# A hybrid attention kernel on one core: most branch gates computed in pairs of seven half-size products

## The chip, the core and the metric

The kernel runs on one core of a Trainium2 chip. TensorE multiplies matrices into PSUM; VectorE, ScalarE and GpSimd work on tiles in SBUF; SyncE issues the loads. The metric is the device time of one execution in microseconds (us). The time before is the median of three runs.

## The reference: what is computed

Two layers of a backbone run over 640 tokens, 512 latent ones and 128 context ones, with a model width of 1024. All data is float32. In each layer

```python
h = rmsnorm(x, norm1_g) * (1 + sc1) + sh1
z = h @ w_in           # pool input, conv inputs, q, k, v, and 3 x 1024 gates
g = sigmoid(gates)     # one gate for each of three branches
merged = (g[:, :, 0] * (pool_out @ w_br_pool)
          + g[:, :, 1] * (conv_out @ w_br_conv)
          + g[:, :, 2] * (attn_out @ w_br_attn))
x = x + g1 * (merged @ w_o)
h2 = rmsnorm(x, norm2_g) * (1 + sc2) + sh2
x = x + g2 * ((silu(h2 @ w_gate) * (h2 @ w_up)) @ w_down)
```

The shifts, scales and gates sh1, sc1, g1, sh2, sc2, g2 are six slices of `silu(c) @ w_ada + b_ada`, 6 x 1024 values per layer and group of tokens.

## The kernel before

Activations lie with channels on the 128 partitions and the 640 tokens along the row, eight chunks of 128 channels. Each float32 operand is held as two parts in TensorE's input form: a rounded high part and the exact rest, the low part. A product of one weight block and one chunk is three matmuls (high by high, low by high, high by low), on two halves of 320 tokens. So a plain output block of 128 channels, eight chunks deep, takes 8 x 2 x 3 = 48 matmuls of 320 columns (`mm`, `mm_op`, L682).

In the feed-forward part, two blocks that read the same input (gate and up) are computed as a *pair* (`Pair`, `Seven`, `product`, L585): the 2 x 2 block product is formed from seven products of half size instead of eight, each 4 chunks x 3 = 12 matmuls. For it the weights are added into four sums s1 to s4 and the input into four sums t1 to t4. Of a pair's seven weight parts three (a11, a12, a22) are the loaded weights themselves and four are sums. `Quarters` holds the input side: `exact` keeps the unsplit input that the norm has just made, `combine` forms t1 to t4 from it on VectorE, and `parts` splits them.

Weights come by SyncE into four raw buffers (`RAW`), are rounded by ScalarE (L351) and get their low part from VectorE by a subtraction (L352), into six buffers `wq` (`WQ`). A plain unit of 1024 columns takes two of these, a half-size part or a branch block one. The 24 gate blocks of a layer (three branches, eight chunks) are plain units in the order `MERGE`. `Merge.gate` takes the tanh of a gate on ScalarE (L1476), multiplies it with the branch's product on VectorE (L1481), adds (L1487) and splits the sum of three (L300, L301) into four of the thirteen big buffers (`BIG`).

From the end of attention on, `ada_back` computes the modulation: for each of 48 rows of `w_ada` in layer 0 and 32 in layer 1 a load of 512 KB and two VectorE instructions with read-out (L751). Two row buffers, `av` and `ap`, lie in room that the attention's values and scores have left; the two conditioning vectors lie in the room of the keys (`k`).

The order of the instructions on every engine is fixed at build time. A planner (`_Order`) runs all these routines as tasks with estimated costs: each engine takes the waiting instruction that is due first. Main work is due at once, weight splits 1.5 us later (`WEIGHT`), weight sums 6 us later, and modulation rows (`BACK`) only where nothing else waits. On the chip each engine runs its list strictly in order.

## Time and profile before

| what | value |
|---|---|
| median of three runs | 1872.57 us (1868.22 to 1874.47) |
| profiled execution | 1872.58 us |
| its span | 1870.5 us |
| TensorE busy | 1820.7 us (97%), 12427 matmuls |
| VectorE busy | 1394.1 us (75%), 2343 instructions |
| ScalarE busy | 816.3 us (44%), 1437 instructions |
| GpSimd busy | 40.1 us (2%), 79 instructions |
| granted clock, mean of the span | 0.993 |
| DMA: bytes moved | 196.81 MB, all loads and stores issued by SyncE |

Busy time is an average over stages with different limits, so the stages are read one by one. Layer 0 ends its attention at about 227 us; the merge with its gates follows up to about 432 us, then `w_o` and the norm, and from 553 us the feed-forward part in four groups (6, 6, 6 and 4 blocks), each followed by eight blocks of `w_down`. Layer 1 starts near 947 us and repeats this.

### The profile page before, as it was taken

The numbers are of one execution on the slowest core, as the hardware profiler recorded it, in microseconds if no ns is written. First come the engines' busy times: TensorE is split into PE (matmuls) and PEld (weight loads), VectorE is DVE, ScalarE is ACT, GpSimd is POOL, SyncE is SP. The second block draws the span as 40 slices with busy tenths as digits, with TensorE's granted clock in tenths as the row PEclk, the third lists the DMA queues.
The fourth block names the chain that finished last, engine by engine and source line by source line (L and its number), as shares of the span: only waits on it lengthen the run. The fifth ranks groups of instructions, "written<-read, shape, count | busy, mean of one in ns | idle before, by whom it ended". The sixth has DMA issues, their size and how long they took to land.

```text
span 1870.5 us, 30822 instructions
## 1 busy us (share of the span) xinstructions
PE 1820.7 (97%) x12427; PEld 1791.5 (96%) x12427; DVE 1394.1 (75%) x2343; ACT 816.3 (44%) x1437; POOL 40.1 (2%) x79
## 2 busy tenths in 40 slices
PE   7999999999999999999999999999999999999997
PEld 4999999999989999999989999999999999999997
DVE  7798778997597684866679987897348858577575
ACT  5587622222454352443466774222226525335244
POOL 0100000000000000000011000000000000000000
PEclk9999999999999999999999999999999999999998
DMA  8210155666212222222332103654331222322222
GB/s 324 84 36 31 56 176 188 201 197 215 77 45 83 80 82 88 79 82 87 90 123 71 43 29 121 197 197 146 99 133 35 80 90 79 90 75 82 82 68 68
DMA packets 65008, 196.81 MB, mean 105 GB/s; under 512 B 7521, under 2 KB 11617, under 8 KB 64865
## 3 DMA queue, kind: packets, MB, share of 16 engines
q1 hardware_dynamic: 64866, 194.85, 31.8%
q8 instruction: 97, 1.59, 0.4%
q14 instruction: 45, 0.37, 0.1%
HBM read 188.01 MB, written 5.51 MB: 103 GB/s over the span
## 4 chain that ended last, share of the span: by engine, by line
PE 74%; DVE 13%; DMA 5%; issue 5%; ACT 2%; POOL 0%; SPq 0%; DVEq 0%; POOLq 0%; ACTq 0%
PE ps L682 41%; PE ps L585 25%; DVE junk L751 4%; DVE wq L352 3%; DMA av<-in_w_ada 3%; DMA ap<-in_w_ada 3%; PE ps L1201 2%; PE ps L1239 2%; PE ps L1219 2%; DVE t L1481 1%; DVE u L1487 1%; PE ps L1674 1%; DVE g L555 1%; PE ps L1010 1%; DVE g L298 1%
## 5 line engine op out<-in xcount | busy, mean ns | idle before, releaser
L682 PE MATMUL ps<-g,wq 128*128 128x320 f32 x7488 | 1145.5, 310 | 11.4 <-DVE wq L352 7.4
L682 PEld LDWEIGHTS ps<-g,wq 128*128 128x128 f32 x7488 | 1105.0, 188 | 16.4 <-DVE wq L352 9.5
L585 PE MATMUL ps<-g,wq 128*128 128x320 f32 x3360 | 500.3, 310 | 7.3 <-DVE wq L352 4.8
L585 PEld LDWEIGHTS ps<-g,wq 128*128 128x128 f32 x3360 | 496.9, 189 | 9.7 <-DVE wq L352 5.6
L351 ACT CAST wq<-wr 128x512 fp32r<-128x512 f32 (+2 forms) x312 | 244.5, 784 | 312.9 <-PE ps L682 242.5
L352 DVE TENSOR_TENSOR wq<-wr,wq 128x512 fp32r<-128x512 f32 (+2 forms) x312 | 277.8, 890 | 80.6 <-ACT wq L351 79.3
L1526 DVE SCALAR_TENSOR_TENSOR g<-ps,mod,g 128x128 f32<-128x128 f32 (+3 forms) x172 | 83.3, 523 | 187.9 <-PE ps L682 187.9
L351 ACT CAST wq<-u 128x512 fp32r<-128x512 f32 x160 | 98.8, 621 | 126.2 <-PE ps L585 60.9
L352 DVE TENSOR_TENSOR wq<-u,wq 128x512 fp32r<-128x512 f32 x160 | 109.1, 687 | 22.9 <-ACT wq L351 22.2
L751 DVE CUSTOM_DVE_ANT_0 junk<-av,k,vec 128x1024 bf16<-128x1024 f32 x80 | 102.5, 1282 | 21.6 <-DMA av<-in_w_ada 20.1
L751 DVE CUSTOM_DVE_ANT_0 junk<-ap,k,vec 128x1024 bf16<-128x1024 f32 x80 | 102.6, 1282 | 12.3 <-DMA ap<-in_w_ada 10.6
L1476 ACT ACTIVATE t<-ps 128x640 f32<-128x640 f32 x32 | 22.6, 705 | 180.4 <-PE ps L682 180.4
L642 ACT COPY t<-ps 128x320 f32<-128x320 f32 x80 | 34.2, 427 | 75.0 <-PE ps L585 75.0
L1209 ACT ACTIVATE pp<-ps,st 128x640 f32<-128x640 f32 x64 | 50.9, 796 | 25.5 <-DVE st L1207 22.7
L298 DVE TENSOR_TENSOR g<-ps,g 128x640 fp32r<-128x640 f32 (+1 forms) x68 | 54.8, 808 | 5.9 <-ACT g L297 5.5
L916 ACT ACTIVATE g<-t,mod,gain 128x320 fp32r<-128x320 f32 (+5 forms) x108 | 55.5, 572 | 6.6 <-DVE t L897 3.3
L297 ACT CAST g<-ps 128x640 fp32r<-128x640 f32 (+1 forms) x68 | 46.4, 684 | 19.9 <-PE ps L1219 16.4
L1207 DVE TENSOR_REDUCE st<-ps 128x1 f32<-128x640 f32 x64 | 52.2, 815 | 3.9 <-PE ps L1201 3.5
L301 DVE SCALAR_TENSOR_TENSOR g<-t,g 128x640 fp32r<-128x640 f32 x44 | 36.2, 823 | 18.5 <-ACT g L300 18.5
L1201 PE MATMUL ps<-k,g 128*128 128x320 f32 x256 | 48.9, 313 | 0.2 <-ACT pp L1209 0.2
L300 ACT ACTIVATE g<-u 128x640 fp32r<-128x640 f32 x16 | 11.8, 739 | 80.7 <-DVE u L1487 80.7
L647 DVE TENSOR_TENSOR t<-t,ps 128x320 f32<-128x320 f32 x80 | 38.7, 484 | 10.9 <-PE ps L585 8.2
(156 smaller groups left out, 1425.1 us busy)
## 6 DMA issues: line engine op xcount, KB each, us to landing
wr<-in_w_in SPq DMA_DIRECT2D x76, 512.0 KB, 3.4
wr<-in_w_gate SPq DMA_DIRECT2D x44, 512.0 KB, 3.3
wr<-in_w_up SPq DMA_DIRECT2D x44, 512.0 KB, 3.3
av<-in_w_ada SPq DMA_DIRECT2D x40, 512.0 KB, 3.7
ap<-in_w_ada SPq DMA_DIRECT2D x40, 512.0 KB, 3.4
wr<-in_w_down SPq DMA_DIRECT2D x48, 384.0 KB, 3.0
g<-in_w_ada SPq DMA_DIRECT2D x16, 512.0 KB, 7.9
wr<-in_w_br SPq DMA_DIRECT2D x32, 256.0 KB, 2.9
```

Of the source, the lines that this page charges most:

```text
L297: yield act(n, lambda: nc.scalar.copy(hi, src))
L298: yield dve(n, lambda: nc.vector.tensor_sub(lo, src, hi))
L351: yield act(n, lambda: nc.scalar.copy(hi, src), slack=WEIGHT)
L352: yield dve(n, lambda: nc.vector.tensor_sub(lo, src, hi), slack=WEIGHT)
L585: nc.tensor.matmul(out, lhsT=wt[q][:, k * P : k * P + P], rhs=x.get(t, lo, k), start=start and k == 0 and i == 0, stop=stop and k == 3 and ...
L682: nc.tensor.matmul(toks(ps, c0, n), lhsT=wt[:, c], rhs=xt[:, c0 : c0 + n], start=start and i == 0, stop=stop and i == 2,)
L751: return dve(n + 60, lambda: nc.vector.tensor_tensor_reduce(out=waste[:, :n], in0=w, in1=s, scale=0.5, scalar=start, op0=ALU.mult, op1=ALU ...
L916: nc.scalar.activation(out, sl, AF.Identity, bias=bias, scale=scale)
L1201: nc.tensor.matmul(toks(ps, c0, n), lhsT=qs, rhs=kt[:, c0 : c0 + n], start=j == 0, stop=j == 1)
L1207: yield dve(TOK, lambda: nc.vector.tensor_reduce(st[:, 0:1], toks(ps), axis=AX.X, op=ALU.max, negate=True))
L1209: yield act(TOK + 140, lambda: nc.scalar.activation(pp, toks(ps), AF.Exp, bias=st[:, 0:1], accum_out=st[:, 1:2]))
L1526: yield dve(n, lambda: nc.vector.scalar_tensor_tensor(xs, toks(ps, s0, n), mods[l][:, v, seg * KC + m : seg * KC + m + 1], xs, op0=ALU.mul ...
```

## The change

- **Gates in pairs.** Of a layer's 24 gate blocks 20 become ten pairs: for each of the chunks 2 to 7 the pool and the conv gate together, then the attention gates of two neighbouring chunks. The pool and conv gates of chunks 0 and 1 (`SINGLE`) stay plain. All attention gates come last, each followed by its branch product.
- **Input sums.** `combine_split` runs when attention is done. The unsplit input of the first norm no longer exists, so it is made again as high + low (8 additions on VectorE), in two big buffers; then t1, t3, t2 and t4 are formed and split.
- **Low parts by adding DMA.** For a11, a12 and a22 of every pair, in the feed-forward part too, ScalarE writes the rounded high part and its negative in the low part's place, and GpSimd issues a DMA that adds the exact weights from DRAM to that negative. The parts s1 to s4 keep the subtraction on VectorE.
- **Room.** Keys and values now share one tile `kv`. After attention it holds the sums of chunks 0 to 3 of the merge and the conditioning vectors; chunks 4 to 7 are summed in a big buffer. The merged sum's own four big buffers are taken two at a time, in the order in which room comes free. The modulation has one row buffer, `p`, left.
- **Modulation rows.** Layer 0 now computes 72 rows (its own 32 and 40 of layer 1), layer 1 only the last 8.

```diff
+KV = 2 * NKV * (PAST + TOK) + 6 * NKV * 2 * HD
+
+SINGLE = 2
...
+    def far_split(hi, lo, src, whence, n, raw_done=None):
+
+        yield act(n, lambda: nc.scalar.copy(hi, src), slack=WEIGHT)
+        yield act(n, lambda: nc.scalar.activation(lo, src, AF.Copy, scale=-1.0), slack=WEIGHT)
+        if raw_done:
+            raw_done.fire()
+        yield _Op({"pool": 1100.0}, lambda e: nc.gpsimd.dma_start(
+            out=lo, in_=whence.bitcast(F32R), accum_op=ALU.add), slack=WEIGHT)
+        yield 4000.0
...
+            (b0, b1), c0, c1 = self.src, slice(0, h), slice(h, D)
+            self.whence = {"a11": b0[:, c0], "a12": b0[:, c1], "a21": b1[:, c0], "a22": b1[:, c1]}
...
-            yield from half_split(self.hi[q], self.lo[q], self.part[q], D // 2)
-            self.parted[q].fire()
+            if q in self.whence:
+                yield from far_split(self.hi[q], self.lo[q], self.part[q], self.whence[q], D // 2, self.parted[q])
+            else:
+                yield from half_split(self.hi[q], self.lo[q], self.part[q], D // 2)
+                self.parted[q].fire()
...
-        MERGE = [(0, 0), (0, 1), (1, 0), (1, 1), (0, 2), (1, 2)]
-        MERGE += [(m, b) for m in range(2, KC) for b in range(3)]
-        for m, b in MERGE:
-            plan.append(Unit(a["w_in"][l, B_G + b * KC + m]))
-            if b != 1:
-                plan.append(Unit(a["w_br"][l, m, :, (b // 2) * 512 : (b // 2) * 512 + 512], 512))
+        for m in range(KC):
+            branch = Unit(a["w_br"][l, m, :, :512], 512)
+            if m < SINGLE:
+                plan += [Unit(gate_of(m, 0)), branch, Unit(gate_of(m, 1))]
+            else:
+                plan += [Pair(gate_of(m, 0), gate_of(m, 1)), branch]
+        for m in range(0, KC, 2):
+            plan.append(Pair(gate_of(m, 2), gate_of(m + 1, 2)))
+            plan += [Unit(a["w_br"][l, m + i, :, 512:], 512) for i in range(2)]
...
+        def combine_split(self):
+
+            yield from self.make()
+            for i in range(2):
+                hi, lo = self.whole.tiles[i], self.whole.tiles[2 + i]
+                for c in range(4):
+                    yield dve(TOK, lambda: nc.vector.tensor_add(
+                        self.z[i][:, c], hi[:, c].bitcast(F32), lo[:, c].bitcast(F32)))
+            b11, b12, b21, b22 = (self.z[i][:, :, j * HA : j * HA + HA] for i in range(2) for j in range(2))
+            done = []
+            for q, out, x, y in (("t1", b11, b12, b11), ("t3", b12, b22, b12), ("t2", b22, b22, b11), ("t4", b21, b21, b22)):
+                for c in (slice(0, 2), slice(2, 4)):
+                    yield dve_any(2 * HA, lambda e: e.tensor_sub(out[:, c], x[:, c], y[:, c]))
+                done.append(spawn(self.parts(q, out)))
...
-    def ada_back(keys_free, todo):
-
-        yield keys_free
+    def ada_back(made, room, todo):
+
+        yield made
...
-        rows = _Slots(order, 2)
+        rows = _Slots(order, 1)
...
-        spaces = [
-            sb.tile([P, 6 * NKV * 2 * HD], F32, tag="v", name=nm("av"))[:, :D],
-            sb.tile([P, 2 * TOK], F32, tag="p", name=nm("ap"))[:, :D],
-        ]
+        spaces = [mk("p", "", (2 * TOK,))[:, :D]]
...
+        def sums(self, i, room):
+            if i:
+                self.sum_slot = yield BIG.get(2)
+                self.room.append(big_t(self.sum_slot, F32))
             else:
+                self.room.append(room[0][:, : 4 * TOK].rearrange("p (a b) -> p a b", a=4))
...
+    def tanh_first(c):
+        yield c.first
+        yield half_tanh(c.x, c.x, TOK)
+        return c.xslot, c.x
...
-            todo = [(l, m) for m in range(2 * KC, NADA)]
-            todo += [(l + 1, m) for m in range(2 * KC) if l + 1 < DEPTH]
-            bg = spawn(ada_back(att.done, todo))
-            after([att.done], lambda x=mg.mg: spawn(x.make()))
+            todo = [(0, m) for m in range(2 * KC, NADA)] + [(1, m) for m in range(5 * KC)]
+            if l:
+                todo = [(1, m) for m in range(5 * KC, NADA)]
...
+            gq = Quarters(h)
+            after([att.done], lambda q=gq: spawn(q.combine_split()))
...
+                c = Seven()
+                spawn(mg.gate(m, 0, tanh_first(c), bs[0]))
+                spawn(mg.gate(m, 1, tanh_second(c), bs[1]))
+                yield from c.run(gq)
+                w = yield from weights()
+                for b in range(2):
+                    yield from branch(m, b, bs[b], w)
+            after([bs[1]["done"]], pc.free)
+            spawn(mg.make())
```

Where it moves instructions is seen at three places. `ps` is a PSUM tile, `g` a big buffer, `wq` a weight buffer; the last number of a name counts tiles.

TensorE in the merge of layer 0, before: the end of a plain attention gate (`ps_346`), its branch product (`ps_351`), and the next plain gate (`ps_356`).

```order
L682 MATMUL ps_346_2667<-g_17_131,wq_338_2576 128x320
L682 MATMUL ps_346_2667<-g_17_131,wq_339_2577 128x320
L682 MATMUL ps_346_2667<-g_19_133,wq_338_2576 128x320
L682 MATMUL ps_351_2732<-g_126_918,wq_344_2653 128x320
L682 MATMUL ps_351_2732<-g_126_918,wq_345_2654 128x320
L682 MATMUL ps_351_2732<-g_128_920,wq_344_2653 128x320
...
L682 MATMUL ps_356_2767<-g_13_127,wq_347_2672 128x320
L682 MATMUL ps_356_2767<-g_13_127,wq_348_2673 128x320
L682 MATMUL ps_356_2767<-g_18_132,wq_347_2672 128x320
```

TensorE, after, at the first pair behind the plain gates: `ps_345`, `ps_350` and `ps_353` collect the seven products, `g_332`, `g_339`, `g_340` and `g_348` are t1 to t4, and L729 is the branch product.

```order
L632 MATMUL ps_345_2693<-g_11_125,wq_327_2517 128x320 x2
L632 MATMUL ps_345_2693<-g_16_130,wq_327_2517 128x320
L632 MATMUL ps_350_2715<-g_332_2578,wq_334_2588 128x320 x12
L632 MATMUL ps_345_2693<-g_340_2663,wq_336_2590 128x320 x12
L632 MATMUL ps_353_2756<-g_15_129,wq_342_2677 128x320 x2
L632 MATMUL ps_353_2756<-g_17_131,wq_342_2677 128x320
...
L632 MATMUL ps_345_2693<-g_339_2620,wq_344_2679 128x320 x12
...
L632 MATMUL ps_345_2693<-g_348_2700,wq_351_2722 128x320 x12
L729 MATMUL ps_366_2842<-g_125_917,wq_352_2740 128x320 x2
```

Where 48 + 48 matmuls stood for two gates there are now seven groups of 12 (rows marked x2 and x12 are repeated), which need the four input sums, and both branch products follow behind them.

VectorE in the second group of the feed-forward part of layer 0, before: the parts of a pair (L352), weight sums (L443), the pair's results gathered from PSUM (L647), and the gating (L1915 to L1921).

```order
L647 TENSOR_TENSOR t_870_7425<-t_870_7425,ps_884_7490 128x320
L352 TENSOR_TENSOR wq_886_7511<-u_868_7401,wq_886_7511 128x512
L443 TENSOR_TENSOR u_887_7527<-wr_883_7478 128x512
L647 TENSOR_TENSOR z_871_7426<-z_871_7426,ps_869_7424 128x320
L352 TENSOR_TENSOR wq_888_7529<-wr_854_7264,wq_888_7529 128x512
L443 TENSOR_TENSOR u_889_7538<-u_887_7527,wr_882_7476 128x512
L647 TENSOR_TENSOR t_870_7425<-t_870_7425,ps_877_7449 128x320
L352 TENSOR_TENSOR wq_890_7547<-u_878_7454,wq_890_7547 128x512
L443 TENSOR_TENSOR u_895_7568<-wr_882_7476,wr_883_7478 128x512
L1915 SCALAR_TENSOR_TENSOR t_891_7557<-t_891_7557,t_870_7425 128x640
L352 TENSOR_TENSOR wq_896_7570<-u_880_7466,wq_896_7570 128x512
L1918 TENSOR_TENSOR t_891_7557<-t_891_7557,z_871_7426 128x320
```

VectorE, after, at the same place: L356 is the split of a sum, L463 a weight sum, L694 the gathering, L2054 and L2057 the gating, and L798 (ISA) a modulation row with its read-out.

```order
L694 TENSOR_TENSOR t_798_6465<-t_798_6465,ps_811_6531 128x320
L798 ISA junk_78,mod1_75<-p_337_2593,kv_307_2399,vec_68 128x1024
L798 ISA mod1_75 128x1
L356 TENSOR_TENSOR wq_814_6555<-u_796_6446,wq_814_6555 128x512
L694 TENSOR_TENSOR z_799_6466<-z_799_6466,ps_797_6464 128x320
L798 ISA junk_78,mod1_75<-p_337_2593,kv_307_2399,vec_68 128x1024
L798 ISA mod1_75 128x1
L694 TENSOR_TENSOR t_798_6465<-t_798_6465,ps_805_6489 128x320
L356 TENSOR_TENSOR wq_817_6592<-u_807_6496,wq_817_6592 128x512
L463 TENSOR_TENSOR u_816_6586<-wr_812_6533 128x512
L2054 SCALAR_TENSOR_TENSOR t_818_6602<-t_818_6602,t_798_6465 128x640
L356 TENSOR_TENSOR wq_822_6614<-u_808_6510,wq_822_6614 128x512
```

The splits of the loaded weights (`wq` from `wr`) have left VectorE, and instructions of the modulation stand in their place, two for a row.

SyncE in the merge of layer 0, before: loads of weights (`wr`) and of modulation rows into `av` and `ap`.

```order
L284 DMA wr_412_3389<-in_w_in 128x1024
L284 DMA av_334_2549<-in_w_ada 128x1024
L284 DMA wr_416_3438<-in_w_br 128x512
L284 DMA ap_335_2550<-in_w_ada 128x1024
L284 DMA wr_422_3501<-in_w_in 128x1024
L284 DMA av_334_2549<-in_w_ada 128x1024
L284 DMA ap_335_2550<-in_w_ada 128x1024
```

SyncE, after, at a like place: one row buffer, `p`.

```order
L288 DMA p_337_2593<-in_w_ada 128x1024
L288 DMA wr_379_2943<-in_w_in 128x1024
L288 DMA p_337_2593<-in_w_ada 128x1024
L288 DMA wr_399_3096<-in_w_in 128x1024
L288 DMA wr_400_3099<-in_w_br 128x512
L288 DMA p_337_2593<-in_w_ada 128x1024
L288 DMA wr_403_3119<-in_w_in 128x1024
```

Before, the rows go to two tiles by turns; now each load into `p` stands behind the reading of the row before it.

## Rows read from the trace of the kernel before

**Rows 1.** which stretches of layer 0 and 1: us, busy us of each engine, PEclk, DMA share, GB/s

```profile
320.00:380.00 60.00, 58.13 (x396) 57.87 (x396) 55.20 (x83) 14.52 (x20) 0.00 (x0) 1.00 0.62 200
380.00:432.00 52.00, 49.09 (x332) 48.30 (x330) 47.25 (x71) 11.64 (x17) 0.00 (x0) 1.00 0.62 203
638.00:712.00 74.00, 74.00 (x507) 74.00 (x506) 59.02 (x99) 38.88 (x70) 0.00 (x0) 1.00 0.26 82
712.00:754.00 42.00, 42.00 (x288) 42.00 (x287) 20.27 (x34) 7.41 (x11) 0.00 (x0) 1.00 0.26 82
1150.00:1281.00 131.00, 128.63 (x874) 127.84 (x873) 113.72 (x168) 30.80 (x41) 0.00 (x0) 1.00 0.59 192
1281.00:1405.00 124.00, 124.00 (x848) 124.00 (x848) 56.39 (x77) 33.03 (x47) 0.00 (x0) 1.00 0.34 115
```

**Rows 2.** chain of waits, feed-forward of layer 0: start us, us, what

```profile
637.60 73.92 PE ps L585 x504
711.52 42.24 PE ps L682 x288
```

**Rows 3.** waits of TensorE in 225 to 432 us: us in total, times, longest

```profile
PE ps L682 <- DVE wq L352: 4.8, 4, 1.9
```

**Rows 4.** timeline of VectorE in the merge: start us, us, engine, line, op, tiles

```profile
248.64 1.28 DVE L751 CUSTOM_DVE_ANT_0 junk<-av,k,vec 128x1024 bf16<-128x1024 f32 x1
249.84 0.08 DVE L751 DVE_READ_ACCUMULATOR2_ANT mod<- 128x1 f32 x1
249.96 1.28 DVE L751 CUSTOM_DVE_ANT_0 junk<-ap,k,vec 128x1024 bf16<-128x1024 f32 x1
...
254.70 1.28 DVE L751 CUSTOM_DVE_ANT_0 junk<-av,k,vec 128x1024 bf16<-128x1024 f32 x1 [2.12 <-DMA av<-in_w_ada]
...
256.51 0.82 DVE L1481 SCALAR_TENSOR_TENSOR t<-t,ps 128x640 f32<-128x640 f32 x1
257.24 1.22 DVE L352 TENSOR_TENSOR wq<-wr,wq 128x1024 fp32r<-128x1024 f32 x1
```

**Rows 5.** VectorE's groups by shape over the span: busy us, mean ns, idle before

```profile
L352 DVE TENSOR_TENSOR wq<-u,wq 128x512 fp32r<-128x512 f32 x160 | 109.1, 687 | 22.9 <-ACT wq L351 22.2
L647 DVE TENSOR_TENSOR t<-t,ps 128x320 f32<-128x320 f32 x80 | 38.7, 484 | 10.9 <-PE ps L585 8.2
L1487 DVE TENSOR_TENSOR u<-u,t 128x640 f32<-128x640 f32 x32 | 26.2, 820 | 0.3
L751 DVE CUSTOM_DVE_ANT_0 junk<-ap,k,vec 128x1024 bf16<-128x1024 f32 x80 | 102.6, 1282 | 12.3 <-DMA ap<-in_w_ada 10.6
L280 DVE TENSOR_SCALAR pp<-pp,st 128x640 f32<-128x640 f32 x33 | 18.2, 552 | 1.0
```

**Rows 6.** timeline at attention's end in layer 0: TensorE's two, VectorE's last

```profile
223.75 1.36 PE L1239 MATMUL ps<-g,vv 128*128 128x256 f32 x10
224.94 37.25 PE L682 MATMUL ps<-g,wq 128*128 128x320 f32 x253
226.44 0.42 DVE L298 TENSOR_TENSOR g<-t,g 64x256 fp32r<-64x256 f32 x1 [0.47 <-ACT g L297]
```

**Rows 7.** ScalarE's group for the weights' high parts over the span

```profile
L351 ACT CAST wq<-u 128x512 fp32r<-128x512 f32 x160 | 98.8, 621 | 126.2 <-PE ps L585 60.9 <-issue 25.1 <-PE ps L682 24.6
```

**Rows 8.** DMA: issues with KB and median us to landing; landings of tile av

```profile
wr<-in_w_br SPq DMA_DIRECT2D x32, 256.0 KB, 2.9
g<-in_w_ada SPq DMA_DIRECT2D x16, 512.0 KB, 7.9
DMA to landing us min/median/max: 3.1/3.7/4.8
```

**Rows 9.** waits of VectorE for modulation rows, 225 to 432 us

```profile
DVE junk L751 <- DMA av<-in_w_ada: 14.5, 9, 3.5
DVE junk L751 <- DMA ap<-in_w_ada: 5.0, 5, 1.9
```

More of the change, by code (lines that the diff above doesn't have):

```diff
@@ L1076, in make @@
             l = self.l
-            kt = [mk("k", g, (2, PAST + TOK), F32R) for g in range(NKV)]
-            self.kk = [[t[:, p, :] for p in range(2)] for t in kt]
-            self.vv = sb.tile([P, 6, NKV, 2 * HD], F32R, tag="v", name=nm("vv"))
+            room = mk("kv", "", (KV,), F32R)
+            n = PAST + TOK
+            self.kk = [[room[:, (2 * g + p) * n : (2 * g + p + 1) * n] for p in range(2)] for g in range(NKV)]
+            self.vv = room[:, 2 * NKV * n :].rearrange("p (t g d) -> p t g d", t=6, g=NKV)
             i = yield TT.get()
@@ L1179, in run @@
             yield self.cache.keys
-            self.pp = sb.tile([P, 2, TOK], F32, tag="p", name=nm("pp"))
+            self.pp = mk("p", "", (2, TOK))
             for hh in range(NH):
@@ L1777, in main, with open_room, branch @@
                     got["there"].fire()
[L1778 to L1793 removed]
+            todo = [(0, m) for m in range(2 * KC, NADA)] + [(1, m) for m in range(5 * KC)]
+            if l:
+                todo = [(1, m) for m in range(5 * KC, NADA)]
+            room, opened = [], event()
+            def open_room(r=room, e=opened, g=mg):
+                r.append(mk("kv", "", (KV,)))
+                e.fire()
+                spawn(g.sums(0, r))
+            after([att.done], open_room)
+            bg = spawn(ada_back(opened, room, todo))
+            gq = Quarters(h)
+            after([att.done], lambda q=gq: spawn(q.combine_split()))
+            parts = (Part(pc, 0), Part(pc, 2), att.ao)
+            def branch(m, b, box, w):
                 box["slot"] = yield PS.get(0)
@@ L1799, in main, with boxes @@
                     after([box["done"]], w.free)
-                if (m, b) == (KC - 1, 1):
-                    after([box["done"]], pc.free)
-                if (m, b) == (KC - 1, 2):
-                    after([box["done"]], att.ao.free)
+            def boxes():
+                return {"there": event()}, {"there": event()}
+            for m in range(KC):
+                if m == 4:
+                    spawn(mg.sums(1, None))
+                bs = boxes()
+                if m < SINGLE:
+                    for b in range(2):
+                        got = yield from plain()
+                        spawn(mg.gate(m, b, tanh_of(*got), bs[b]))
+                        if not b:
+                            w = yield from weights()
+                        yield from branch(m, b, bs[b], w)
+                    continue
+                c = Seven()
+                spawn(mg.gate(m, 0, tanh_first(c), bs[0]))
+                spawn(mg.gate(m, 1, tanh_second(c), bs[1]))
+                yield from c.run(gq)
+                w = yield from weights()
+                for b in range(2):
+                    yield from branch(m, b, bs[b], w)
+            after([bs[1]["done"]], pc.free)
+            spawn(mg.make())
+            for m in range(0, KC, 2):
+                bs = boxes()
+                c = Seven()
+                spawn(mg.gate(m, 2, tanh_first(c), bs[0]))
+                spawn(mg.gate(m + 1, 2, tanh_second(c), bs[1]))
+                used = yield from c.run(gq)
+                for i in range(2):
+                    w = yield from weights()
+                    yield from branch(m + i, 2, bs[i], w)
+            after([used], gq.free)
+            after([bs[1]["done"]], att.ao.free)
             x = Stream()
@@ L1811, in main @@
             after([h.made], lambda q=hq: spawn(q.make()))
-            done = yield from with_norm(l, 1, 2, x, mg.mg, KC, stats, h, quarters=hq)
-            after([done], mg.mg.free)
+            done = yield from with_norm(l, 1, 2, x, mg, KC, stats, h, quarters=hq)
+            after([done], mg.free)
             after([done], lambda q=hq: spawn(q.combine()))
```

115 lines of the change are left out of this document (76 added, 39 removed).

## The prediction

> **What bounds the kernel now.** First the stages: the table of stretches [rows 1] takes parts of layer 0 (320 to 754 us) and of layer 1, and one reads TensorE's column (PE) against the length. In the feed-forward part TensorE is busy for all of 74.00 and 42.00 us; in the branch merge of layer 0 it loses 1.87 us of 60 and 2.91 us of 52, in that of layer 1 2.37 us of 131 and then nothing. The chain of waits [rows 2] gives the price of a product: 504 products of 320 columns in 73.92 us, 288 in 42.24 us, 146.7 ns each in either form of the code (the 310 ns that a row shows overlap). The granted clock there is 1.00, the higher of the two levels, 2.4 GHz. The waits of TensorE [rows 3] name what it loses in the merge: 4.8 us, in 4 waits, for weights that VectorE (DVE) was late to split. So the end is set by the count of products, and next by VectorE, which is busy for 55.20 of 60 us and 47.25 of 52 us there [rows 1], and 59.02 of 74 us in the feed-forward part. ScalarE (ACT) has room everywhere.
>
> **The change part by part**, against the profiled run (1872.58 us, span 1870.5, so 2.1 us outside it; the median of the three is 1872.57).
>
> *Products.* A pair of plain gates is 2 x 48 products; seven half-size products are 7 x 12 = 84. 20 gates a layer are 10 pairs, 20 pairs in all: 20 x 12 x 0.1467 = **-35.2 us**, on the path as long as TensorE stays fed.
>
> *VectorE in the merge.* For output chunks 2 to 7 a step is 84 + 24 products, 15.84 us. VectorE's list for it holds 9 instructions of 512 columns (4 weight sums, 4 low parts, one branch weight), 3 sums of 320 from PSUM, 3 of 640 (two gates, one add), and two modulation rows of two L751 each. Row durations are 0.687, 0.484, 0.820 and 1.282 us [rows 5]; in a full stretch [rows 4] each starts 0.08 us before its neighbour ends (256.51 to 257.24 is 0.73 for a 0.82), and an L751 with its read-out takes 1.32 (248.64 to 249.96). So 9 x 0.61 + 3 x 0.40 + 3 x 0.74 + 4 x 1.32 = 14.2 us, 89% of the step. The attention steps come to 16.9 of 19.36 us (two branch weights, two adds, two splits more), 87%. Both lie just under the 91 to 92% at which 4.8 us of 112 were lost. 172.5 us of this in layer 0 lose between 0 and 172.5 x 4.8/112 = 7.4 us; I take 4, near the upper row, and the old 4.8 go. In layer 1 only 8 modulation rows are left where 32 stood, a step's list falls below 9 us, and I take 0.5 for the old 2.4. **-3 us**, from -7 to +2.
>
> *Quarter sums for the first pair.* They start when attention is done: its last VectorE piece starts at 226.44 us, while TensorE goes on at 224.94 with plain gate work [rows 6]. By the order 207 products follow before the first pair, 30.4 us, to 255.3; its first product needs no sums, the second (257.1) needs t1, the third (258.8) t2. VectorE's list up to t1 is 24 us from 226.9, to 250.6; t2 comes some 7 us later, behind a gate that itself waits for TensorE until 255.6: 257.5 to 259. It meets 258.8 from either side: **+2 us** for two layers, from 0 to 5.
>
> *Into w_o.* Chunks 4 to 7 of the merged sum are now split only after the last pair has freed its room. Behind the last branch stand one gate (0.74) and three low parts, while w_o asks for chunk 4 after 12 products, 1.76 us: **+1 us** for two layers, 0 to 2.
>
> *Low parts by adding DMA.* Of each pair's seven parts three lose their VectorE subtraction; ScalarE gets a second copy, and GpSimd issues a DMA that adds the weights in. 10 + 20 pairs a layer, 180 of them. Their cover is the ring of six weight buffers: a buffer freed by one product serves the sixth after it, so five products, 5 x 12 x 0.1467 = 8.8 us, lie between. Two ScalarE copies take 2 x 0.62 [rows 7]; some 7.3 us are left for hand-offs, issue and flight. No row of this kernel shows such a DMA or any issued by GpSimd. From below: a plain load of the same 256 KB lands in 2.9 us [rows 8]. From above: the 512 KB loads of the start, queued behind each other, take 7.9. The transfer is small and the queue is not full, so I stand near the lower row, doubled at most because the destination is read too: under 6 us, inside the cover, **0**. ScalarE's list for a feed-forward pair grows to some 9 of 12.32 us, which is free.
>
> *VectorE in the feed-forward part of layer 0.* 18 low parts per group leave it, but modulation rows come in: 72 rows are now done in layer 0 (48 before), some 45 of them behind w_o. One group is 73.92 + 42.24 = 116.2 us. VectorE was busy for 59.02 + 20.27 = 79.3 us of it [rows 1]; minus 18 x 0.61, plus 16 rows x 2 x 1.32 = 42.2, is 110.5 us (107 by start-to-start times). And there is one row buffer where there were two: a row's load can only start when the row before is read, so VectorE waits out what its list between two rows doesn't fill. Those gaps hold 1.7 to 3.7 us of work in most of the 16 places; a row lands 3.1 to 4.8 us after issue, median 3.7 [rows 8]. At 3.5 (single loads, not two behind one another) the waits add about 13 us a group, at 3.1 about 8, at 4.1 about 20. So VectorE needs 115 to 127 us where TensorE needs 116: up to 11 too many in each of 2.8 groups, of which the weight ring and PSUM take up some 6 us once. From 0 to 20 us; I take 3.5 and so **+8 us**. TensorE had no wait there before, so lighter splits bring nothing.
>
> Sum: 1872.6 - 35.2 - 3 + 2 + 1 + 0 + 8 = 1845.4, say **1845 us**.
>
> A rule of the Trainium skill speaks against the adding DMA. First the rows: of the VectorE forms on 640 columns one, the scaling by a scalar (L280), takes 552 ns where a two-tensor form takes 820 [rows 5]; L280 belongs to attention, and neither pairs nor merge use it. The Trainium skill (SBUF — State Buffer, Who interferes with whom) says that descriptor generation on GpSimd is locked out for the length of a VectorE instruction in a two-port mode, which copies and tensor-by-scalar forms enter and two-tensor forms don't. By that rule nothing in the pairs locks it, and the sum stays; if all VectorE forms did, each issue would wait for at most the instruction that runs, 1.28 us, which the 7.3 us still cover.
>
> **Rivals.** (1) *VectorE is late nowhere*: row loads land in 3.1 us, the merge loses nothing: 1872.6 - 35.2 - 7 + 1 = 1831 at the very best, 1836 with the small terms as taken. For it: VectorE has the 11 us a group of the low parts back. Against: one row buffer. (2) *Row loads bind in layer 0*: landings of 4.1 us, as 249.96 to 254.7 and its like in the old merge suggest, cost 20 us instead of 8 and the merge its 7.4: 1861. For it: the 19.5 us that VectorE waited for rows in the old merge although two buffers stood there [rows 9]. Against: with one buffer two rows never share the engines. (3) *The adding DMA is late, and the kernel slower*: where issue and flight take more than 7.3 us, each further us delays TensorE once for each turn of the ring, about once a pair: 60 us per us over 60 pairs. It decides from 0.45 us over, 7.8 us, since 27 us are there to be eaten; at 8.3 us the time is 1845 + 60 = 1905. For it: the destination is read and written, GpSimd shares the queue with loads, and there is no row of one. Against: 2.9 us for the same bytes. (4) *The pairs come late*, their quarters or weights held back by VectorE in both merges so that TensorE idles what it saved: VectorE would have to be 20% over the 14.2 us; 1870.
>
> **How the numbers follow.** About 0.3%, 5.6 us, is what a measurement of this kernel tells from no change. Forecast (1840 to 1852) 0.50; rival 1 (1831 to 1840) 0.20; rival 2 (1852 to 1866) 0.14; rival 4 and a mildly late DMA (1867 to 1878) 0.06; rival 3 (above 1878) 0.10. Faster by over 0.3%: 0.50 + 0.20 + 0.14 = 0.84; within 0.06; slower 0.10. The range leaves out rivals 3 and 4 and the edge of rival 1: 1834 to 1866.
>
> **What would show it.** Right: 240 products fewer in the trace, merges of layer 1 at 146.7 ns a product, no wait of TensorE in the feed-forward part of layer 1, waits of VectorE for the rows' tile (p) of some 30 to 40 us in layer 0, TensorE's losses in layer 0 behind weights that VectorE split. Wrong: waits of TensorE for a DMA into the weight buffers, in both layers alike (rival 3); gaps before the first pair longer than 3 us; feed-forward groups of layer 0 at 116.2 us (rival 1) or above 124 (rival 2).

## The result and the profile after

The changed kernel takes 1883.79 us (median of 4 runs, 1882.18 to 1889.22) against 1871.43 us of the kernel before in the same comparison: 1.0073 times as long, 95% interval 1.0057 to 1.0089. It is slower by 12 us where the prediction said faster by 27. Its profiled run is the longest of the four (1889.22 us, span 1887.5); that of the kernel before had a span of 1870.5, so the traces show 17 us to be explained (the medians 12), and these are 35 us that were saved and 52 that were lost.

The saving is there. The chain of waits of the changed kernel in layer 1 (start us, us, what) answers to [rows 2]:

```profile
1215.87 12.31 PE ps L632 x84
1228.19 3.52 PE ps L729 x24
...
1516.96 42.24 PE ps L729 x288
1559.20 73.92 PE ps L632 x504
```

A pair of gates is 84 products in 12.31 us, where two plain gates took 96, and the feed-forward part of layer 1 runs at the old 146.7 ns a product. The losses show in a table of stretches, which answers to [rows 1]. First the kernel before, then the changed one; each has four rows: merge and output projection of layer 0, the feed-forward part of layer 0 with the norm's tail ahead of it, and the same two of layer 1. The columns are start and end, length, busy time and count of PE, PEld, DVE, ACT and POOL, granted clock, DMA share, GB/s:

```profile
224.94:499.33 274.39, 269.61 (x1835) 268.56 (x1833) 216.66 (x320) 69.39 (x97) 0.00 (x0) 1.00 0.54 179
518.70:945.26 426.56, 421.77 (x2848) 419.40 (x2846) 301.62 (x513) 180.79 (x321) 0.00 (x0) 0.99 0.26 82
1137.79:1404.66 266.87, 264.50 (x1802) 263.71 (x1800) 176.07 (x253) 67.98 (x95) 0.00 (x0) 1.00 0.47 154
1424.02:1849.59 425.57, 420.78 (x2847) 418.52 (x2845) 299.90 (x510) 185.56 (x332) 0.00 (x0) 1.00 0.23 72
```

```profile
225.96:489.91 263.95, 255.66 (x1715) 253.52 (x1713) 219.96 (x348) 122.99 (x225) 26.60 (x30) 0.99 0.61 178
509.27:976.24 466.97, 438.09 (x2850) 430.06 (x2848) 371.30 (x639) 210.47 (x382) 52.31 (x60) 0.97 0.60 159
1168.64:1421.88 253.24, 248.82 (x1682) 247.65 (x1680) 173.76 (x270) 120.90 (x222) 26.20 (x30) 0.99 0.54 144
1441.24:1866.41 425.17, 421.35 (x2847) 419.59 (x2845) 265.40 (x450) 214.54 (x392) 52.30 (x60) 0.99 0.47 110
```

The merges are shorter by 10.4 and 13.6 us, although 120 products fewer are worth 17.6 each. The feed-forward part of layer 1 is as long as before. That of layer 0 is **40.4 us longer** with the same products. Two things are in these 40 us. TensorE idles 28.9 us of the stretch (466.97 less 438.09), where it was 4.8. And the same products keep it busy for 16.3 us more, at a mean granted clock of 0.97. One such place, at the start of a group's down projection (stretches in the same columns):

```profile
720.00:725.20 5.20, 1.56 (x11) 1.27 (x9) 4.40 (x10) 1.73 (x3) 0.00 (x0) 1.00 0.68 195
725.16:728.57 3.41, 3.18 (x13) 2.85 (x12) 3.27 (x6) 0.83 (x1) 0.00 (x0) 0.51 0.24 95
728.60:732.00 3.40, 3.40 (x25) 3.40 (x25) 1.74 (x4) 0.00 (x0) 0.00 (x0) 0.99 0.63 190
```

TensorE stands idle for most of 5 us, and then the granted clock is 0.51 (the lower level, 1.2 GHz) for 3.4 us: 13 products where 25 run in the next 3.4. What it waited for is in the timeline of that place (start us, us, engine, line, op, tiles, in brackets the idle time before and what ended it):

```profile
713.02 0.08 DVE L798 DVE_READ_ACCUMULATOR2_ANT mod<- 128x1 f32 x1
...
713.13 0.33 SPq L288 DMA_DIRECT2D p<-in_w_ada  x1
...
717.73 1.28 DVE L798 CUSTOM_DVE_ANT_0 junk<-p,kv,vec 128x1024 bf16<-128x1024 f32 x1 [2.97 <-DMA p<-in_w_ada]
718.94 0.08 DVE L798 DVE_READ_ACCUMULATOR2_ANT mod<- 128x1 f32 x1
718.94 0.48 DVE L694 TENSOR_TENSOR t<-t,ps 128x320 f32<-128x320 f32 x1
719.34 0.95 DVE L356 TENSOR_TENSOR wq<-wr,wq 128x768 fp32r<-128x768 f32 x1
...
723.58 0.48 DVE L2060 TENSOR_TENSOR t<-t,ps 128x320 f32<-128x320 f32 x1
724.09 0.74 ACT L304 ACTIVATE g<-t 128x640 fp32r<-128x640 f32 x1 [3.10 <-DVE t L2060]
...
724.88 0.63 PE L729 MATMUL ps<-g,wq 128*128 128x320 f32 x2 [3.64 <-ACT g L304]
```

VectorE stands for 2.97 us at a modulation row that has not landed (tile `p`). SyncE issued its load at 713.13, as soon as the row before was read, so the wait is the flight of the load and not a late issue. VectorE's instructions run in a fixed order, so the sums from PSUM (L694), the split weights (L356) and the last gating of the group (L2060) come that much later, ScalarE's copy behind them too, and TensorE idles 3.64 us. The row names "ACT g L304" for this wait, but ScalarE itself waited for VectorE, and VectorE for the DMA. Over the feed-forward part of layer 0 half of TensorE's waits end like that, at VectorE's sums from PSUM: the first line below (us in all, times, longest). The second has VectorE's waits for rows in the same part, the third those over the program:

```profile
PE ps L632 <- DVE z L694: 13.9, 7, 4.9
DVE junk L798 <- DMA p<-in_w_ada: 55.8, 35, 3.9
DVE junk L798 <- DMA p<-in_w_ada: 79.3, 50, 4.0
```

77.2 of the 79.3 us lie in layer 0 (21.4 in its merge, 55.8 in its feed-forward part), where the prediction looked for 30 to 40.

### The profile page after: what moved, and what is told of

It is laid out like the page before. It is cut to its first block, busy times and chain, and to the rows that moved or that the text cites. A ratio compares the mean times of both kernels' runs of the same rounds, so it can differ in the third digit from the quotient of the medians.

```text
span 1887.5 us, 31398 instructions
## 1 busy us (share of the span) xinstructions
PE 1809.1 (96%) x12187; PEld 1772.5 (94%) x12187; DVE 1429.2 (76%) x2452; ACT 980.3 (52%) x1812; POOL 197.7 (10%) x259
## 3 DMA queue, kind: packets, MB, share of 16 engines
q1 hardware_dynamic: 64866, 194.85, 31.1%
q0 software_dynamic: 25920, 47.20, 15.7%
## 4 chain that ended last, share of the span: by engine, by line
PE 67%; DVE 15%; DMA 10%; issue 5%; ACT 3%; POOL 0%; SPq 0%; DVEq 0%; POOLq 0%; ACTq 0%
PE ps L729 34%; PE ps L632 25%; DMA p<-in_w_ada 8%; DVE junk L798 4%; DVE wq L356 2%; PE ps L1246 2%; PE ps L1284 2%; PE ps L1264 2%; DVE u L463 1%; PE ps L1780 1%; DVE g L602 1%; DVE g L305 1%; DMA wq<-in_w_in 1%; PE ps L1054 1%; DVE g L302 0%
## 5 line engine op out<-in xcount | busy, mean ns | idle before, releaser
L729 PE MATMUL ps<-g,wq 128*128 128x320 f32 x5568 | 873.2, 312 | 13.2 <-ACT g L304 7.3
L729 PEld LDWEIGHTS ps<-g,wq 128*128 128x128 f32 x5568 | 829.0, 189 | 19.2 <-ACT g L304 8.8
L632 PE MATMUL ps<-g,wq 128*128 128x320 f32 x5040 | 766.8, 313 | 34.1 <-DVE z L694 18.5
L798 DVE CUSTOM_DVE_ANT_0 junk<-p,kv,vec 128x1024 bf16<-128x1024 f32 x160 | 205.0, 1281 | 80.9 <-DMA p<-in_w_ada 79.3
L355 ACT CAST wq<-u 128x512 fp32r<-128x512 f32 x240 | 147.6, 620 | 190.3 <-issue 57.9
L355 ACT CAST wq<-wr 128x1024 fp32r<-128x1024 f32 (+2 forms) x152 | 128.0, 845 | 199.7 <-PE ps L729 164.2
L356 DVE TENSOR_TENSOR wq<-u,wq 128x512 fp32r<-128x512 f32 x240 | 162.4, 686 | 49.1 <-ACT wq L355 49.1
L356 DVE TENSOR_TENSOR wq<-wr,wq 128x1024 fp32r<-128x1024 f32 (+2 forms) x152 | 146.6, 966 | 30.4 <-ACT wq L355 29.4
L360 ACT CAST wq<-wr 128x512 fp32r<-128x512 f32 x180 | 112.0, 622 | 77.7 <-PE ps L632 40.6
L364 POOL DMA_DIRECT2D wq<-in_w_gate x80 | 69.8, 872 | 477.8 <-ACT wq L361 259.0
L361 ACT ACTIVATE wq<-wr 128x512 fp32r<-128x512 f32 x180 | 113.4, 630 | 0.0
L364 POOL DMA_DIRECT2D wq<-in_w_in x60 | 52.8, 880 | 472.7 <-ACT wq L361 164.8
L694 DVE TENSOR_TENSOR t<-t,ps 128x320 f32<-128x320 f32 x120 | 58.1, 484 | 27.3 <-PE ps L632 24.5
L1254 ACT ACTIVATE p<-ps,st 128x640 f32<-128x640 f32 x64 | 51.0, 797 | 25.6 <-DVE st L1252 22.8
L301 ACT CAST g<-ps 128x640 fp32r<-128x640 f32 (+1 forms) x68 | 46.4, 684 | 19.9 <-PE ps L1264 16.3
```

The source lines that it names most:

```text
L355: yield act(n, lambda: nc.scalar.copy(hi, src), slack=WEIGHT)
L356: yield dve(n, lambda: nc.vector.tensor_sub(lo, src, hi), slack=WEIGHT)
L360: yield act(n, lambda: nc.scalar.copy(hi, src), slack=WEIGHT)
L361: yield act(n, lambda: nc.scalar.activation(lo, src, AF.Copy, scale=-1.0), slack=WEIGHT)
L364: yield _Op({"pool": 1100.0}, lambda e: nc.gpsimd.dma_start(out=lo, in_=whence.bitcast(F32R), accum_op=ALU.add), slack=WEIGHT)
L632: nc.tensor.matmul(out, lhsT=wt[q][:, k * P : k * P + P], rhs=x.get(t, lo, k), start=start and k == 0 and i == 0, stop=stop and k == 3 and ...
```

## The experiments

Each run is compared with the kernel before on the same chip. Three theories stood at the start: (1) VectorE stands at rows that land late; (2) VectorE's list is too long whatever the loads do; (3) the adding DMAs are late themselves. The table gives for each run the median and, from its trace, what TensorE lost in each of the four stretches: their length less the count of products of 320 columns (1830, 2844, 1797 and 2841 before; 120 fewer in each changed merge, 12 of them back with a third plain chunk) times 0.14667 us. The trace is that of one run, so a row need not add up to the median beside it.

| run | us | merge 0 | feed-forward 0 | merge 1 | feed-forward 1 |
|---|---|---|---|---|---|
| before | 1871.4 | 6.0 | 9.4 | 3.3 | 8.9 |
| changed | 1883.8 | 13.1 | 49.8 | 7.3 | 8.5 |
| e1 no row loads | 1839.6 | 6.6 | 9.0 | 7.0 | 6.9 |
| e2 second row buffer | 1858.5 | 12.9 | 21.8 | 8.0 | 8.5 |
| e3 48 and 32 rows | 1875.1 | 9.8 | 29.4 | 12.6 | 12.6 |
| e4 GpSimd subtracts | 1911.8 | 15.6 | 64.0 | 13.4 | 12.4 |
| e5 no adding DMAs | 1847.4 | 2.1 | 22.5 | 6.7 | 7.0 |
| e6 = e2 with e3 | 1855.6 | 13.4 | 12.1 | 13.6 | 7.2 |
| e7 = e6, third plain chunk | 1850.6 | 9.1 | 9.6 | 7.3 | 7.1 |
| e8 before, one row buffer | 1885.7 | 7.5 | 11.3 | 8.6 | 9.7 |
| e9 before, adding DMAs | 1868.7 | 6.2 | 7.0 | 2.5 | 6.8 |
| e10 before, both | 1894.3 | 10.5 | 17.5 | 11.6 | 9.2 |
| e11 = e7 without adding DMAs | 1839.3 | 2.4 | 12.0 | 2.0 | 8.8 |
| e12 = e7, rows 1 us later | 1843.0 | 4.7 | 12.4 | 6.7 | 7.8 |

**e1: the waits for rows taken away, their work kept.**

```diff
-                yield dma(w, a["w_ada"][l, m], follow=True, done=ld[1])
+                f = dma(w, a["w_ada"][l, m], follow=True, done=ld[1])
+                if (l, m) != todo[0]:
+                    f.fn = lambda e: None
+                yield f
```

> The changed kernel (1883.8 us; its feed-forward part of layer 0 takes 420.5 us for 373.1 us of products) with every modulation row's load left out but the first of a layer, so that all rows multiply the same data: each engine keeps its order and VectorE all its 160 reductions, and only the waiting for rows and their traffic go. Theory 1 (VectorE stands in its fixed order at a row that has not landed, with one row buffer, and the weights behind it come late): that part falls to 380 to 388 us, the merge of layer 0 gets some 5 us back, in all 1836 to 1850. Theory 2 (VectorE's list is too long for TensorE, whatever the loads do): the part stays above 405 us, in all above 1865. Theory 3 (the adding DMAs are late on their own account): waits of TensorE for them stay, in all above 1870.

1839.62 us, 0.9836 (0.9821 to 0.9851) of the kernel before: theory 1. The feed-forward part takes 379.7 us by the measure of the expectation, just below its range. VectorE's list is as long as in the changed kernel, and the feed-forward part of layer 0 loses no more than it did before the change. Theory 2 falls.

**e5: the adding DMAs taken away, the rows kept.**

```diff
-        yield _Op({"pool": 1100.0}, lambda e: nc.gpsimd.dma_start(
-            out=lo, in_=whence.bitcast(F32R), accum_op=ALU.add), slack=WEIGHT)
+        yield _Op({"pool": 1100.0}, lambda e: None, slack=WEIGHT)
```

> The changed kernel with the 180 adding DMAs left out (the low parts stay the negated weights); the order of every engine and all other work stay. It asks what the 47 MB of adding DMAs do to the row loads, which land after 4.3 us (median) in the changed kernel and after 3.7 in the kernel before. Theory A (the adding DMAs share the DMA engines with the rows and so make VectorE's waits longer): rows land after some 3.3 us, VectorE's waits for them fall from 79 to about 40 us, the feed-forward part of layer 0 loses 25 to 35 us in place of 50, the first pair of layer 0 starts without its 3 us: in all 1852 to 1868. Theory B (the one row buffer alone makes the waits): VectorE waits 70 us or more, in all 1872 to 1882.

1847.44 us, 0.9881 (0.9864 to 0.9898): theory A, and stronger than expected (the part loses 22.5 us, 25 to 35 were said). So either can be taken away, the rows' loads or the adding DMAs, and most of the loss is gone. What ties them together is read from one feed-forward group of layer 0, the second, in three kernels. The stretches, from the first product of the pairs to the last of the down projection, of the changed kernel, of e5 and of e1:

```profile
633.93:764.68 130.75, 122.34 (x794) 119.98 (x793) 102.97 (x175) 55.00 (x98) 15.69 (x18) 0.96 0.64 172
```

```profile
614.22:735.30 121.08, 117.00 (x795) 116.22 (x794) 103.95 (x180) 55.38 (x98) 0.00 (x0) 1.00 0.44 145
```

```profile
618.46:735.30 116.84, 116.55 (x795) 116.19 (x794) 105.34 (x180) 55.24 (x98) 15.66 (x18) 1.00 0.52 122
```

and VectorE's waits for rows with the landing times of tile `p` in the first, then in the second (in the third there are none):

```profile
DVE junk L798 <- DMA p<-in_w_ada: 22.9, 13, 3.9
DMA to landing us min/median/max: 3.2/4.7/6.4
```

```profile
DVE junk L797 <- DMA p<-in_w_ada: 14.0, 12, 2.6
DMA to landing us min/median/max: 3.1/3.3/5.2
```

VectorE's work is 103 to 105 us in all three. With rows that land after 4.7 us it waits 22.9 us, and work and waits are 126 of the group's 131 us; with rows after 3.3 us they are 118 of 121; without waits TensorE's 116.8 us stand alone. This is the group that suffers most: the four groups are 5.9, 14.6, 13.2 and 6.7 us longer than before the change. Over the whole feed-forward part of layer 0, landing times and waits of the changed kernel and then of e5 are

```profile
DMA to landing us min/median/max: 3.1/3.8/6.8
  DMA p<-in_w_ada: 55.8, 35
```

```profile
DMA to landing us min/median/max: 3.1/3.3/5.2
  DMA p<-in_w_ada: 37.3, 34
```

Beside the adding DMAs a row lands later, by 1.4 us in the median of that group and by 0.5 over the part, and VectorE, with one row buffer, waits 18.5 us more for 44 rows. The Trainium skill (DMA: Bandwidth & Descriptors, Issuing engines are not separate DMA queues) says that transfers started by different engines run on the same 16 DMA engines and interleave; the two landing times agree with it.

**e2: a second row buffer where one comes free.** Late in the merge the columns that held the sums of chunks 0 to 3 fall idle.

```diff
-    def ada_back(made, room, todo):
+    def ada_back(made, room, todo, more):
...
+        after(more, lambda: rows.put(1))
...
-        spaces = [mk("p", "", (2 * TOK,))[:, :D]]
+        spaces = [mk("p", "", (2 * TOK,))[:, :D], room[0][:, :D]]
...
-            bg = spawn(ada_back(opened, room, todo))
+            bg = spawn(ada_back(opened, room, todo, [mg.ev[0][m] for m in range(4)]))
```

> The changed kernel with a second row buffer from the end of the merge on, in the columns of the keys' room that held the sums of chunks 0 to 3; nothing is added to any engine's work. Theory 1: the feed-forward part of layer 0 falls from 420.5 to 385 to 398 us, the merge is as it was, in all 1848 to 1862. Theory 2: the same list on VectorE, so 1878 to 1890. Theory 3: the same as theory 2.

1858.52 us, 0.9935 (0.9918 to 0.9952). The feed-forward part of layer 0 gets 28 of its 40 us back with all adding DMAs in place, and VectorE's waits for rows there fall from 55.8 to 5.3 us; the merges lose what they lost. The buffer opens at 403 us, late in the merge of layer 0, so 7 of the 44 rows move ahead of the part. By e3, where 24 rows fewer are worth 20.4 us, that is some 6 of the 28, an estimate.

**e3: 24 rows moved back to layer 1.**

```diff
-            todo = [(0, m) for m in range(2 * KC, NADA)] + [(1, m) for m in range(5 * KC)]
-            if l:
-                todo = [(1, m) for m in range(5 * KC, NADA)]
+            todo = [(l, m) for m in range(2 * KC, NADA)]
+            todo += [(l + 1, m) for m in range(2 * KC) if l + 1 < DEPTH]
```

> The changed kernel with the modulation rows shared out as in the kernel before: 48 in layer 0 and 32 in layer 1 in place of 72 and 8. Behind the output projection of layer 0 stand some 21 rows in place of 45. Theories 1 and 2 alike: the feed-forward part of layer 0 loses about half of what it lost, 47 to some 25 us, and the merge of layer 1 loses as much as that of layer 0 (13 in place of 7 us): in all 1862 to 1870. Theory 3: the loss goes with the pairs and not with the rows, in all 1878 to 1890.

1875.07 us, 1.0028 (1.0012 to 1.0043): between the two ranges, in neither. Layer 0 did what was expected (29.4 lost in place of 49.8) and the merge of layer 1 too (12.6); that the rows cost another 4 us in the feed-forward part of layer 1 was not reckoned with. By the traces the run is 16.8 us below the changed kernel, by the medians 8.7: the trace of the changed kernel is of its longest run. The run also shows that a group need not be full for a late row to cost: in its second group VectorE's work and row waits are 91.2 and 16.8 of 133.0 us, and the group still loses 16.9 us; its 9 rows all stand in the first 88 us.

**e4: GpSimd subtracts in place of the adding DMAs.**

```diff
-        yield act(n, lambda: nc.scalar.activation(lo, src, AF.Copy, scale=-1.0), slack=WEIGHT)
+        yield _Op({"act": 0.83 * n + 70}, lambda e: None, slack=WEIGHT)
...
-        yield _Op({"pool": 1100.0}, lambda e: nc.gpsimd.dma_start(
-            out=lo, in_=whence.bitcast(F32R), accum_op=ALU.add), slack=WEIGHT)
+        yield _Op({"pool": 1100.0}, lambda e: nc.gpsimd.tensor_sub(lo, src, hi), slack=WEIGHT)
```

> The changed kernel with each adding DMA replaced by a subtraction on GpSimd at the same place of its list, and the negating ScalarE copy left out: 47 MB of traffic go, and 180 subtractions of 512 columns come. Theory 3 (the adding DMAs delay the row loads, landing after 4.8 us in the merge in place of 3.7, and the first pair): row loads land a us earlier and the first pair loses no 3 us to a landing, in all 1850 to 1866 if a subtraction takes under 4 us. Theory 1 alone with row loads as late as now: 1875 to 1885. Theory 2: 1880 to 1890. If GpSimd takes over 7 us for one, or holds VectorE up, all are slower than 1890.

1911.79 us, 1.0221 (1.0206 to 1.0236). Rows land sooner (median 3.3 us), but VectorE is held up. Its groups by shape over the span (busy us, mean ns, idle before), the changed kernel's and then those of e4:

```profile
L463 DVE TENSOR_TENSOR u<-wr,u 128x512 f32<-128x512 f32 x60 | 41.0, 683 | 0.0
L694 DVE TENSOR_TENSOR t<-t,ps 128x320 f32<-128x320 f32 x120 | 58.1, 484 | 27.3 <-PE ps L632 24.5
```

```profile
L462 DVE TENSOR_TENSOR u<-wr,u 128x512 f32<-128x512 f32 x60 | 64.1, 1068 | 0.0
L693 DVE TENSOR_TENSOR t<-t,ps 128x320 f32<-128x320 f32 x120 | 57.7, 481 | 17.9 <-PE ps L631 16.4
L797 DVE CUSTOM_DVE_ANT_0 junk<-p,kv,vec 128x1024 bf16<-128x1024 f32 x160 | 220.5, 1378 | 39.5 <-DMA p<-in_w_ada 38.0
```

The sum of two SBUF operands that is hit most goes from 683 to 1068 ns, the rows' reduction from 1281 to 1378, and a sum with one operand in PSUM stays at 481. That is the rule of the Trainium skill (SBUF — State Buffer, Who interferes with whom) that a VectorE instruction with two SBUF inputs contends with a GpSimd instruction that reads SBUF. This run therefore doesn't isolate the adding DMAs; e5 does.

**e8, e9, e10: the two parts in the kernel before.** One row buffer (`_Slots(order, 1)`); three low parts of each of its 40 feed-forward pairs by adding DMA; both.

```diff
-        rows = _Slots(order, 2)
+        rows = _Slots(order, 1)
```

```diff
-            yield from half_split(self.hi[q], self.lo[q], self.part[q], D // 2)
-            self.parted[q].fire()
+            if q in self.whence:
+                yield from far_split(self.hi[q], self.lo[q], self.part[q], self.whence[q], D // 2, self.parted[q])
+            else:
+                yield from half_split(self.hi[q], self.lo[q], self.part[q], D // 2)
+                self.parted[q].fire()
```

> The kernel before (1869.7 us) with one row buffer in place of two and nothing else changed. If one buffer is enough to make VectorE late: its waits for rows grow from some 20 to over 40 us in the merge of layer 0, the rows reach into the feed-forward part, and the time is 1876 to 1892. If it takes the adding DMAs or the 24 rows more to make it late: 1867 to 1873.

> The kernel before (1870 us) with one part of the change alone: in its 40 feed-forward pairs three low parts of each come by adding DMA, 120 in all; gates, rows and both row buffers stay as they were. If the adding DMAs hurt only through row loads, and rows are not scarce here with two buffers: 1865 to 1874. If they cost on their own, by landing late for TensorE: over 1876, with waits of TensorE for them in both layers.

> The same with one row buffer. One buffer alone made the kernel before 15 us slower (1885.7). If the two work on one another (the traffic makes rows land later, one buffer makes VectorE stand through each landing): 1890 to 1910, with row loads landing after 4 us or more in place of 3.3. If the 120 subtractions taken off VectorE make up for it: 1872 to 1886.

1885.68 us (1.0080, 1.0065 to 1.0095), 1868.67 us (0.9983, 0.9974 to 0.9993) and 1894.29 us (1.0124, 1.0104 to 1.0145). The adding DMAs alone cost nothing on balance, and VectorE has 120 subtractions fewer; but all rows of e9 stand in the merges, where this kernel has no adding DMAs, so the run does not show what the two do to one another with two buffers (e2 does). One buffer alone costs 15 us, with VectorE's waits for rows at 153.5 us; both together cost 23. The waits in e8 and in e10:

```profile
DVE junk L751 <- DMA av<-in_w_ada: 153.5, 67, 4.6
```

```profile
DVE junk L766 <- DMA av<-in_w_ada: 166.1, 67, 4.5
```

A microsecond waited is not a microsecond lost: 147.7 us of the waits in e8 lie in the merges, where TensorE loses only 6.8 us more than before; with 34 rows in place of 48 VectorE works 178.3 of 275.9 us in the merge of layer 0. The size in e10 came as expected, but the reason given for it shows in one stage only. Its rows land after 3.4 us in the median, not 4, since most of them stand in the merges. In the feed-forward part of layer 0, where the last 14 rows meet adding DMAs, they land after 3.7 us (3.2 in e8), VectorE waits 18.0 us for them in place of 5.8, and TensorE loses 17.5 us in place of 11.3. By the traces each merge loses some 3 us more as well; how, without an adding DMA there, is left open.

**e6, e7, e11, e12: towards a better version.** e6 joins e2 and e3; e7 sets `SINGLE = 3`; e11 is e7 with VectorE subtracting all low parts (`if q in self.whence:` becomes `if False:`); e12 is e7 with `yield 1000.0` ahead of each row's products.

> The second row buffer behind the merge (1858.5 us) together with the old sharing out of the rows, 48 in layer 0 and 32 in layer 1. If rows cost time where VectorE has little room and none where it has much: the feed-forward part of layer 0 loses 10 to 14 us in place of 21.8, the merge of layer 0 some 10 in place of 12.9, the merge of layer 1 some 12.5 in place of 8.0, in all 1846 to 1856. If each row costs the same wherever it stands: 1856 to 1862.

> The same with three chunks of plain gates ahead of the first pair in place of two: 24 products more in the two layers together, 3.5 us. In the changed kernel the first pair of a merge took 16.9 and 18.0 us for 12.3 us of products. If it comes too early for its quarter sums and weights: that loss, 10.3 us for both layers, goes, and the time is 4 to 7 us below that of the run with two chunks. If what it waits for moves along with it (a copy on ScalarE that stands behind a gate's tanh): 2 to 4 us above.

> The version with two row buffers behind the merge, rows 48 and 32, and three chunks of plain gates (1850.6 us), with VectorE subtracting all low parts as in the kernel before: no adding DMAs, 180 subtractions of some 0.61 us more on VectorE, 110 us over the program. If the adding DMAs cost more by late rows than they spare: 1838 to 1848. If VectorE then has too little room in the merges, where it is busiest: 1853 to 1868.

> The version with two row buffers behind the merge, rows 48 and 32, and three chunks of plain gates (1850.6 us), with each row's products put 1.0 us later in VectorE's order by the planner; no other change. If VectorE's standing at rows still costs time there: its waits fall from 31 to some 15 us, 1842 to 1849. If the products then stand in the way of other work, or the waits cost nothing any more: 1849 to 1858.

e6: 1855.64 us (0.9913, 0.9898 to 0.9929), at the upper edge; the merge of layer 0 did not gain. e7: 1850.63 us (0.9901, 0.9879 to 0.9922), whose interval overlaps e6's, so the 5 us are not established as a whole, but the trace shows the first pairs: 14.0 and 14.4 us where they took 16.7 and 17.4 (12.3 both in e11). e12: 1843.04 us (0.9844, 0.9826 to 0.9862), VectorE's waits for rows down from 34.4 to 20.2 us. **e11: 1839.25 us, 0.9828 (0.9813 to 0.9842)**, the fastest that leaves no part of the computation out: 32 us below the kernel before, and its 216 products fewer are worth 31.7. The low parts of 58 pairs, 174 subtractions, went back to VectorE, whose busy time rises by 95.9 us (1423.3 to 1519.2), the adding DMAs and ScalarE's 174 negating copies went, and the kernel became 11 us faster.

## Why the prediction was wrong, point by point

- **Products, -35.2 us: right.** 240 products fewer, at 146.7 ns wherever TensorE is fed.
- **VectorE in the feed-forward part of layer 0, +8 us: this step failed; it was 40.4 us.** The busy time was about right (107 to 110 us for a group said, 103 to 108 measured in the two full groups with rows), and so was the mechanism, one row buffer. The term that was mis-sized is the wait for rows. The prediction took a landing of 3.5 us from plain loads of the kernel before [rows 8] and argued that with one buffer "two rows never share the engines". It overlooked that the same change puts 180 adding DMAs on those engines. Without them its reckoning nearly holds: in e5 rows land after 3.3 us, a group waits 14.0 us for them (13 was said), and the part is 13.1 us longer than before (8 was said, 0 to 20). With them the waits are 22.9 us in the worst group and 55.8 in the part, where 2.8 groups of 13 us make 36. That leaves 27.3 us, which came with the adding DMAs: later rows, more of the lower clock behind TensorE's gaps, and TensorE's own waits for adding DMAs; how it is shared among them is not shown. The sign that the prediction named was half right: TensorE waited for VectorE, but mostly for sums from PSUM (13.9 us) and the gating behind them, and only 2.4 us for weights.
- **The clock, not in the sum at all.** The products of that stretch took 16.3 us more in TensorE's time. This is not 16 us beside the rest: work and row waits of VectorE fill 126 of a group's 131 us, so that in this group at most the 5 us left could come from VectorE waiting for a slower TensorE. How much of the fall is added and how much only fills TensorE's own wait stays open.
- **The adding DMAs, 0 us for TensorE: nearly right, and wrong in effect.** They land after 3.6 to 7.9 us, median 5.0; three of the 180 take longer than the 7.3 us of cover (7.6, 7.7 and 7.9). TensorE waits for them seven times, 3.3 us in the merge of layer 0 and 3.0 in its feed-forward part, and not once in layer 1; with the rows' loads gone (e1) the waits in the feed-forward part are gone too. The larger price came through another queue: the profile lists the adding DMAs and the loads as two queues, where the prediction spoke of one that GpSimd shares. What rival 3 priced (each us over is paid once a pair) did not happen.
- **Merges, first pairs and w_o, 0 us together: +11.1 us** (7.2 in layer 0, 4.0 in layer 1). The first pairs are 10.3 of it, 16.9 and 18.0 us for 12.3 us of products; +2 was said. In layer 0 the prediction looked at the quarter sums, but an adding DMA ended the gap; in layer 1 it was the quarter sums (L602), as described. The rest nearly cancels: the merge of layer 0 is some 2.5 us worse beside its first pair, that of layer 1 some 1.7 better. TensorE's first pairs in the changed kernel, layer 0 and layer 1 (columns as in the timeline above):

```profile
256.32 5.59 PE L632 MATMUL ps<-g,wq 128*128 128x320 f32 x37
264.88 8.48 PE L632 MATMUL ps<-g,wq 128*128 128x320 f32 x47 [2.97 <-DMA wq<-in_w_in]
```

```profile
1199.52 1.14 PE L632 MATMUL ps<-g,wq 128*128 128x320 f32 x6 [1.38 <-DVE g L602]
1202.92 9.43 PE L632 MATMUL ps<-g,wq 128*128 128x320 f32 x52 [2.27 <-DVE g L602]
```

  That DMA was issued at 258.64 and landed at 264.8: its two ScalarE copies stood behind a gate's tanh that itself waited 4.29 us for TensorE. So part of the cover was spent before the DMA was issued. In e5, without the DMAs, the first pair of layer 0 takes 12.32 us and that of layer 1 still 17.7; in e1, without the rows' loads, they take 17.0 and 17.9.
- **The rivals.** Rival 2 (row loads bind in layer 0) was the right one, with 0.14 and 1861 us, priced at a landing of 4.1 us and with the merge at its bound; its evidence, 19.5 us of waits in the old merge with two buffers [rows 9], deserved more. The slower side had only rival 3, whose mechanism was another: no rival let two parts of the change act on one another. They do: a second buffer alone (e2) gives 28 of the 40 us back, 24 rows fewer (e3) 20, and no adding DMAs (e5) 27, which is more than there is to share. Rival 1's 1836 is 1837 by the terms as taken.

The sum with measured terms: -35.2 + 40.4 + 11.1 - 0.4 = +15.9 of the 17.0 us between the two spans.

## What to carry to other kernels

When a change adds traffic and also takes away a buffer, price the wait at that buffer with landing times under the new traffic, not with those of the old trace: without that traffic 27 of the 40 us went (e5), with a second buffer 28 (e2). An instruction that waits for a DMA in an in-order queue delays all that stands behind it, so low-priority work should either be double-buffered or be put into the order later than its load lands on a bad day. Work taken off an engine is worth nothing if that engine loses the time to waits; here 96 us of VectorE's work, given back together with the end of the adding DMAs, made the kernel 11 us faster.

## What the runs showed of the hardware

The kinds of DMA in the changed kernel (packets, MB, share of 16 engines' span; the first row are SyncE's loads, the second GpSimd's adding DMAs):

```profile
q1 hardware_dynamic: 64866, 194.85, 31.1%
q0 software_dynamic: 25920, 47.20, 15.7%
```

A byte that an adding DMA moves keeps the DMA engines busy 2.1 times as long as a plain one (15.7% for 47.2 MB, 31.1% for 194.85). GpSimd is busy 0.87 us to issue one, 1.05 at most. VectorE's instructions are not slower beside them (the rows' reduction takes 1281 ns, 1282 before), but they are beside GpSimd's own subtractions (1378). And an idle time of TensorE of 3.64 us, in a part of the program in which it is otherwise busy for 94% of the time, was followed by 3.4 us at the lower level of the clock; with its like it brought the mean granted clock of 467 us down to 0.97, with 30.7 us at half speed by the trace's clock records (6.8 before). A shorter gap, of 2.27 us at 854 us, was followed by 3.4 us of it too.
